# One Exp and a Newton step for the recurrence's 1/(1+t), and Tanh for all gate sigmoids but one

## The chip, the cores and the metric

The kernel runs on one core of one Trainium2 chip. The metric is device time in microseconds for one execution, 943.13 us as the median of three runs before the change (942.66 to 943.2). The core's engines each have a queue that goes in order: PE multiplies matrices (its weight loads, PEld, run beside it), ACT (ScalarE) evaluates activation functions and copies, DVE (VectorE) does elementwise work, POOL (GpSimd) small operations, SP issues the DMA transfers.

## The reference

A trunk of two layers over 512 positions of width 1024, all in float32. The first ("even") layer projects x once and feeds two branches: eight heads of retention and eight blocks of an RG-LRU recurrence. Each is multiplied by a SiLU gate. The second ("odd") layer is differential attention. The part that matters here:

```python
    ret = ((ret - mu) * lax.rsqrt(var + NORM_EPS)).reshape(B, S, RET_WIDTH) * gn_g + gn_b
    ret = ret * jax.nn.silu(g_ret.astype(jnp.float32))
    lru = rg_lru_branch(xb, conv_w, conv_b, wa, ba, wx, bx, lam) * jax.nn.silu(g_lru.astype(jnp.float32))
...
    r = jax.nn.sigmoid(jnp.einsum('bsgi,gij->bsgj', xg, wa).reshape(B, S, W) + ba)
    i = jax.nn.sigmoid(jnp.einsum('bsgi,gij->bsgj', xg, wx).reshape(B, S, W) + bx)
    log_a = -LRU_C * r * jax.nn.softplus(-lam.astype(jnp.float32))
    a = jnp.exp(log_a)
    u = xc * i * jnp.sqrt(-jnp.expm1(2.0 * log_a))
```

followed by the scan h = a h + u along the positions.

## The kernel before

Every float32 matrix product is three products of a high and a low part (`mm3`): the high part of an operand is a cast on ACT (L145), the low part the difference on DVE (L146), and both have to be there before PE can use the operand. Weights come in pieces of 512 KB through two raw buffers: SP issues a transfer when the piece two before it has been split (its DVE operation, as w19l, is done), ACT and DVE split it (w21h, w21l), PE uses it.

The even layer runs over heads. For each head there are projections for the two gates (`gl`, `gr`), the recurrence's input (`xb`), and retention's q and k, each 24 products of 512 columns on PE. Between these products stand the small ones of the heads: retention's scores (`rs`, four per head), their product with v (`ro`), the GroupNorm's variance (`rv`, which reads the split square `rq`), and the recurrence's two gates (`pr` and `pi`, which read the split convolution `xc`). PE's and SP's order is the order of the program, with turns counted in `Side`; ACT's and DVE's order is laid out by the scheduler, by priorities and its own costs, and is fixed when the program is built. Scores and gates (`rs`, `pr`, `pi`) take turns in two PSUM banks, so a product waits until DVE or ACT has read the one two before it.

The recurrence writes a = exp(log_a) with t = tanh(-log_a / 2): a = (1 - t) / (1 + t) and sqrt(1 - a^2) = 2 sqrt(t) / (1 + t). Its steps on ACT are Sigmoid (L491, into `t`), Sigmoid (L495, into `xbp`), Tanh (L497), Ln of 1 + t (L502), Exp of its negative (L503), Sqrt of t (L506); DVE sharpens 1/(1+t) by a Newton step (L504, L505) and goes on with L507 to L510, the last being the scan. The GroupNorm takes Ln (L461), Exp (L462) and a Square (L463). The gates take a Sigmoid (L408) and a product (L409). Where a function is not in the table set that ACT has loaded, an ACT_TABLE_LOAD stands ahead of it under the same line.

Of the kernel before, what the change touches and what calls it, by code (L numbers as in the profile page):

```python
# [95 lines left out]
def trunk(ctx: ExitStack, tc: tile.TileContext, a):  # L96
# [27 lines left out]
    def temp(name):  # L124
        return es.tile([P, S], F32, tag="es", name=name)
# [247 lines left out]
    conv_w = lambda i, c: vecs[:, i, c:c + 1]  # L373
    conv_b = lambda c: vecs[:, 4, c:c + 1]
    gba = lambda c: vecs[:, 5, c:c + 1]
    gbx = lambda c: vecs[:, 6, c:c + 1]
    gn = load("gn", [P, 2, KT], a["gn"])
    gng = const.tile([P, KT], F32, tag="gng", name="gng")
    nc.vector.tensor_scalar(out=gng, in0=gn[:, 0], scalar1=-0.5, scalar2=None, op0=ALU.mult)
    sg = load("sg", [P, 2], a["subln"])  # L380
    nc.vector.tensor_scalar(out=sg, in0=sg, scalar1=1.0 - LAMBDA_INIT, scalar2=None, op0=ALU.mult)
    cos = load("cos", [P, S], a["cos"])
# [48 lines left out]
    def retention(h, q, k, v, dec, m):  # L431
# [26 lines left out]
        with tc.high_priority(P_GROUP):  # L458
            sd = temp(f"rsd{h}")

            nc.scalar.activation(out=sq, in_=pv, func=AF.Ln, bias=epsb)  # L461
            nc.scalar.activation(out=sd, in_=sq, func=AF.Exp, scale=-0.5)  # L462
            nc.scalar.activation(out=sq, in_=sd, func=AF.Square)  # L463
            nc.vector.scalar_tensor_tensor(out=sq, in0=pv, scalar=EPS, in1=sq, op0=ALU.add, op1=ALU.mult)
            nc.vector.scalar_tensor_tensor(out=sd, in0=sq, scalar=3.0, in1=sd, op0=ALU.subtract, op1=ALU.mult)
            n1 = sq
            nc.vector.tensor_tensor(out=n1, in0=ps, in1=sd, op=ALU.mult)
            nc.vector.tensor_scalar(out=n1, in0=n1, scalar1=gng[:, h:h + 1], scalar2=gn[:, 1, h:h + 1], op0=ALU.mult, op1=ALU.add)
        if ("gr", h) not in gates:
            yield lambda: ("gr", h) in gates  # L470
        nc.vector.tensor_tensor(out=n1, in0=n1, in1=gates.pop(("gr", h)), op=ALU.mult)
# [2 lines left out]
    def lru(c, ps, m):  # L474
# [17 lines left out]
        pi = bank(ps_sc, "sc", f"pi{c}")  # L492
        mm3(pi, cut(gw[0], ALL, slice(o + P, o + 2 * P)), t2, True, True)
        i = xb
        nc.scalar.activation(out=i, in_=pi, func=AF.Sigmoid, bias=gbx(c))  # L495

        nc.scalar.activation(out=t, in_=t, func=AF.Tanh, scale=sp4[:, c:c + 1])  # L497
        nc.vector.tensor_tensor(out=i, in0=i, in1=xc, op=ALU.mult)  # L498
        d = xc
        r = temp(f"r{c}")  # L500

        nc.scalar.activation(out=r, in_=t, func=AF.Ln, bias=1.0)  # L502
        nc.scalar.activation(out=r, in_=r, func=AF.Exp, scale=-1.0)  # L503
# [29 lines left out]
    for kind, i in ev:  # L533
# [256 lines left out]
```

## Time and profile before

| what | value |
|---|---|
| median of the runs | 943.13 us |
| the profiled execution | 943.21 us |
| its span | 941.4 us |
| PE busy | 923.9 us, 98% |
| DVE busy | 692.7 us, 74% |
| ACT busy | 463.6 us, 49% |
| share of PE in the chain that ended last | 64% |
| share of DVE, of ACT in that chain | 19%, 8% |

The span is what the profiler recorded of the program's instructions, and 1.8 us of the execution lie outside of it. The even layer takes the first 400 us or so, the odd layer the rest. Times in rows are from the span's start.

### The profile page before, as it was taken

What the parts mean: (1) busy time and instruction counts of PE and PEld (TensorE: products, weight loads), DVE (VectorE), ACT (ScalarE), POOL (GpSimd) and SP (SyncE); (2) the same over time, 40 slices, a digit from 0 to 9 for tenths busy, and PEclk for the clock granted to TensorE, in tenths of its full rate; (3) what the DMA queues carried; (4) which work ended last, traced back from release to release, by engine and by line L of the source; (5) the groups of instructions that cost most, each with busy time, mean ns of one, the idle gap of its engine ahead of it and who ended that gap; (6) DMA issues with size and microseconds to landing.
All of it is one profiled execution on the core that took longest, in us unless ns stands there. A gap on an engine that the chain in (4) does not pass through costs nothing.

```text
span 941.4 us, 11566 instructions
## 1 busy us (share of the span) xinstructions
PE 923.9 (98%) x4327; PEld 764.8 (81%) x4327; DVE 692.7 (74%) x1171; ACT 463.6 (49%) x750; POOL 58.6 (6%) x118
## 2 busy tenths in 40 slices
PE   9999999999999999999999999999999999999996
PEld 7888888878887887888887888888788888887885
DVE  5877997868779988994489854478844488636777
ACT  5567786566374776423334454233453234444340
POOL 0000000000000000000001210100100001101023
PEclk9999999999999999999999999999999999999998
DMA  6562221512314123314221222042223142223102
GB/s 225 174 218 68 90 73 54 165 57 93 120 54 148 57 90 118 120 29 162 93 89 65 69 89 90 23 134 90 68 68 90 45 135 68 73 85 113 66 23 91
DMA packets 27418, 88.95 MB, mean 94 GB/s; under 512 B 3425, under 2 KB 3553, under 8 KB 27361
## 3 DMA queue, kind: packets, MB, share of 16 engines
q1 hardware_dynamic: 27360, 88.20, 28.6%
q8 instruction: 34, 0.56, 0.2%
q14 instruction: 24, 0.19, 0.1%
HBM read 86.09 MB, written 2.10 MB: 94 GB/s over the span
## 4 chain that ended last, share of the span: by engine, by line
PE 64%; DVE 19%; ACT 8%; issue 4%; DMA 2%; POOL 2%; SPq 0%; DVEq 0%; ACTq 0%; POOLq 0%
PE ov_ps L150 3%; PE ov_ps L151 3%; PE ov_ps L149 3%; PE og_ps L149 3%; PE og_ps L150 3%; PE og_ps L151 3%; PE ev_ps L149 2%; PE ev_ps L150 2%; PE oo_ps L149 2%; PE oo_ps L150 2%; PE oo_ps L151 2%; PE ev_ps L151 2%; ACT e L610 1%; PE xb_ps L149 1%; PE xb_ps L150 1%
## 5 line engine op out<-in xcount | busy, mean ns | idle before, releaser
L610 ACT ACTIVATE e<-as,nm 128x128 f32<-128x128 f32 (+3 forms) x64 | 33.2, 523 | 29.2 <-DVE nm L607 28.8
L641 DVE SCALAR_TENSOR_TENSOR o<-po,ars,og 128x256 f32<-128x256 f32 x32 | 15.5, 484 | 39.8 <-POOL ars L326 39.8
L607 DVE CUSTOM_DVE_ANT_0 as<-as,mask 128x128 f32<-128x128 f32 (+3 forms) x64 | 30.2, 510 | 1.9 <-PE as L151 1.9
L617 POOL TENSOR_SCALAR zr<-z 128x1 f32<-128x1 f32 x32 | 11.3, 352 | 309.9 <-ACT e L610 309.9
L325 POOL TENSOR_SCALAR rs_t<-bmv 128x1 f32<-128x1 f32 x6 | 2.3, 376 | 418.4 <-DVE bmv L336 418.4
L637 ACT ACTIVATE po<-po 128x256 f32<-128x256 f32 x32 | 11.8, 370 | 29.8 <-PE po L151 25.9
L325 POOL TENSOR_SCALAR rs_t<-ss,zr 128x1 f32<-128x1 f32 x32 | 16.0, 501 | 140.5 <-ACT po L637 135.5
L239 DVE TENSOR_TENSOR y<-oo_ps,y 128x512 f32<-128x512 f32 x24 | 16.3, 684 | 4.2 <-PE oo_ps L151 4.2
L326 POOL TENSOR_TENSOR ars<-rs_t,nhalf 128x1 f32<-128x1 f32 x32 | 18.9, 591 | 2.7
L482 DVE SCALAR_TENSOR_TENSOR xc<-xbp,vecs,xc 128x509 f32<-128x509 f32 (+2 forms) x24 | 17.9, 746 | 1.5 <-ACT xc L479 1.3
L618 DVE SCALAR_TENSOR_TENSOR e<-e,zr,e 128x128 f32<-128x128 f32 (+3 forms) x32 | 17.6, 551 | 1.0
L439 DVE TENSOR_TENSOR rsd<-rs,dec 128x512 f32<-128x512 f32 (+3 forms) x32 | 15.5, 486 | 1.1 <-PE rs L151 1.0
L615 DVE RECIPROCAL zr<-z 128x1 f32<-128x1 f32 x32 | 5.2, 162 | 15.1 <-ACT e L610 14.9
L646 PEld LDWEIGHTS po<-ident,o 128*128 128x128 f32 x64 | 8.3, 140 | 7.8 <-DVE o L641 4.8
L646 PE MATMUL po<-ident,o 128*128 128x128 f32 x64 | 12.6, 278 | 1.6 <-DVE o L641 1.4
L622 PE MATMUL wt<-ident,e 128*128 128x128 f32 x80 | 14.0, 272 | 0.0
L145 ACT CAST hh<-ht 128x512 fp32r<-128x512 f32 x8 | 4.7, 588 | 18.4 <-PE ht L577 18.4
L622 PEld LDWEIGHTS wt<-ident,e 128*128 128x128 f32 x80 | 10.4, 140 | 3.8 <-DVE e L618 0.4
L498 DVE TENSOR_TENSOR xbp<-xbp,xc 128x512 f32<-128x512 f32 x8 | 5.5, 690 | 9.9 <-ACT xbp L495 9.9
L610 ACT ACTIVATION_READ_ACCUMULATOR e<-as,nm 128x1 f32 x64 | 12.5, 196 | 0.0
L504 DVE SCALAR_TENSOR_TENSOR xc<-t,r 128x512 f32<-128x512 f32 x8 | 5.5, 691 | 9.0 <-ACT r L503 9.0
L408 ACT ACT_TABLE_LOAD x9 | 11.5, 1283 | 0.8 <-PE gl_ps L151 0.7
(2673 smaller groups left out, 3416.3 us busy)
## 6 DMA issues: line engine op xcount, KB each, us to landing
w_r<-in_od_w SPq DMA_DIRECT2D x64, 512.0 KB, 3.3
w_r<-in_ev_w SPq DMA_DIRECT2D x47, 512.0 KB, 3.3
w_r<-in_ev_wo SPq DMA_DIRECT2D x16, 512.0 KB, 3.4
w_r<-in_od_wo SPq DMA_DIRECT2D x16, 512.0 KB, 3.3
dec<-in_dec SPq DMA_DIRECT2D x8, 256.0 KB, 3.9
y<-in_x SPq DMA_DIRECT2D x4, 512.0 KB, 6.8
out_h<-y SPq DMA_DIRECT2D x8, 256.0 KB, 2.1
xr<-in_xt SPq DMA_DIRECT2D x3, 512.0 KB, 6.7
```

Of the source, the lines that this page charges most:

```text
L149: nc.tensor.matmul(out=out, lhsT=l[0], rhs=r[0], start=start, stop=False)
L150: nc.tensor.matmul(out=out, lhsT=l[0], rhs=r[1], start=False, stop=False)
L151: nc.tensor.matmul(out=out, lhsT=l[1], rhs=r[0], start=False, stop=stop)
L239: nc.vector.tensor_tensor(out=yy, in0=ps, in1=yy, op=ALU.add)
L325: nc.gpsimd.tensor_scalar(out=t, in0=var, scalar1=scale, scalar2=eps, op0=ALU.mult, op1=ALU.add)
L326: nc.gpsimd.tensor_tensor(out=out, in0=t, in1=nhalf[:, :1], op=ALU.pow)
L482: nc.vector.scalar_tensor_tensor(out=xc[:, sh:], in0=xb[:, :S - sh], scalar=conv_w(w, c), in1=xc[:, sh:], op0=ALU.mult, op1=ALU.add)
L607: nc.vector.tensor_tensor_reduce(out=ps[:, :n], in0=ps[:, :n], in1=mask[:, S - n:], scale=-QK_SCALE, scalar=3.0e38, op0=ALU.add, op1=ALU.m ...
L610: nc.scalar.activation(out=e, in_=ps[:, :n], func=AF.Exp, scale=-1.0, bias=nm, accum_out=z[:, mp:mp + 1])
L618: nc.vector.scalar_tensor_tensor(out=ee[0], in0=ee[1], scalar=zr[:, 0:1], in1=ee[0], op0=ALU.mult, op1=ALU.add)
L622: nc.tensor.transpose(out=pt[:, kb * P:kb * P + P], in_=ee[0][:, kb * P:kb * P + P], identity=ident)
L646: nc.tensor.transpose(out=pm[:, i * P:i * P + P], in_=o[:, i * P:i * P + P], identity=ident)
```

## The change

The gates' SiLU, x sigmoid(x), becomes x (1 + tanh(x/2)), which is twice of it; the factor of two is taken out of the GroupNorm's scale and offset (`gng`, `gnb`) and of the recurrence's factor (-2 becomes -0.5, with the one of the input gate `i`, which is formed in the same way, as (1 + tanh) xc). The recurrence's own gate stays a Sigmoid. The start of the Newton step for 1/(1+t), which was exp(-ln(1+t)), becomes (1 + exp(-2 sp4 r)) / 2, which is the same number: an Exp of the Sigmoid's output, scaled, and a Copy that halves it and adds a half. Three small tiles (`sp8`, `gbx2`, `gnb`) are made at the start.

```diff
-    nc.vector.tensor_scalar(out=gng, in0=gn[:, 0], scalar1=-0.5, scalar2=None, op0=ALU.mult)
+    nc.vector.tensor_scalar(out=gng, in0=gn[:, 0], scalar1=-0.25, scalar2=None, op0=ALU.mult)
...
-    def silu(ps, out, name):
+    sp8 = const.tile([P, KT], F32, tag="sp8", name="sp8")
+    nc.vector.tensor_scalar(out=sp8, in0=sp4, scalar1=-2.0, scalar2=None, op0=ALU.mult)
+    gbx2 = const.tile([P, KT], F32, tag="gbx2", name="gbx2")
+    nc.vector.tensor_scalar(out=gbx2, in0=vecs[:, 6], scalar1=0.5, scalar2=None, op0=ALU.mult)
+    gnb = const.tile([P, KT], F32, tag="gnb", name="gnb")
+    nc.vector.tensor_scalar(out=gnb, in0=gn[:, 1], scalar1=0.5, scalar2=None, op0=ALU.mult)
+
+    def silu2(ps, out, name):
+
         s = work(name + "_sg")
-        nc.scalar.activation(out=s, in_=ps, func=AF.Sigmoid)
-        nc.vector.tensor_tensor(out=out, in0=ps, in1=s, op=ALU.mult)
+        nc.scalar.activation(out=s, in_=ps, func=AF.Tanh, scale=0.5)
+        nc.vector.scalar_tensor_tensor(out=out, in0=s, scalar=1.0, in1=ps, op0=ALU.add, op1=ALU.mult)
...
-        nc.scalar.activation(out=i, in_=pi, func=AF.Sigmoid, bias=gbx(c))
-
+        nc.scalar.activation(out=i, in_=pi, func=AF.Tanh, scale=0.5, bias=gbx2[:, c:c + 1])
+
+        r = temp(f"r{c}")
+        nc.scalar.activation(out=r, in_=t, func=AF.Exp, scale=sp8[:, c:c + 1])
         nc.scalar.activation(out=t, in_=t, func=AF.Tanh, scale=sp4[:, c:c + 1])
-        nc.vector.tensor_tensor(out=i, in0=i, in1=xc, op=ALU.mult)
+        nc.vector.scalar_tensor_tensor(out=i, in0=i, scalar=1.0, in1=xc, op0=ALU.add, op1=ALU.mult)
         d = xc
-        r = temp(f"r{c}")
-
-        nc.scalar.activation(out=r, in_=t, func=AF.Ln, bias=1.0)
-        nc.scalar.activation(out=r, in_=r, func=AF.Exp, scale=-1.0)
+
+        nc.scalar.activation(out=r, in_=r, func=AF.Copy, scale=0.5, bias=0.5)
...
-        nc.vector.scalar_tensor_tensor(out=r, in0=r, scalar=-2.0, in1=d, op0=ALU.mult, op1=ALU.mult)
+        nc.vector.scalar_tensor_tensor(out=r, in0=r, scalar=-0.5, in1=d, op0=ALU.mult, op1=ALU.mult)
```

Lines after the new ones move by six. What the queues hold changes at places far from the diff, since the scheduler lays ACT and DVE out anew. Before, on ACT at head 2's recurrence: xc2h is the high part of the convolution, which PE's `pr` reads; w21h that of a weight piece for the output product; r12h and r13h those of retention's scores.

```order
L145 CAST w20h<-w_r 128x1024
L145 CAST r12h<-rsd_1028 128x256
L408 ACTIVATE gr_sg<-gr_ps 128x512
L145 CAST xc2h<-xc_1006 128x512
L145 CAST w21h<-w_r 128x1024
L145 CAST r13h<-rsd_1063 128x128
L491 ACTIVATE t_1088<-pr_1084,vecs 128x512
L497 ACTIVATE t_1088<-t_1088,sp_183 128x512
L495 ACTIVATE xbp_1004<-pi_1090,vecs 128x512
L502 ACT_TABLE_LOAD
L502 ACTIVATE r_1097<-t_1088 128x512
```

With the change, at the same place on ACT:

```order
L145 CAST w20h<-w_r 128x1024
L414 ACTIVATE gr_sg<-gr_ps 128x512
L145 CAST r12h<-rsd_1034 128x256
L145 CAST w21h<-w_r 128x1024
L145 CAST xc2h<-xc_1012 128x512
L145 CAST r13h<-rsd_1069 128x128
L497 ACT_TABLE_LOAD
L497 ACTIVATE t_1094<-pr_1090,vecs 128x512
L504 ACT_TABLE_LOAD
L504 ACTIVATE r_1101<-t_1094,sp_212 128x512
L501 ACTIVATE xbp_1010<-pi_1096,gbx_214 128x512
L505 ACTIVATE t_1094<-t_1094,sp_183 128x512
```

The cast w21h has moved ahead of xc2h, and the gate's Sigmoid has a table load of its own.

Before, on ACT at head 7's recurrence: `rq` is the square of the sixth head's GroupNorm, k7h the high part of the seventh head's k.

```order
L491 ACT_TABLE_LOAD
L491 ACTIVATE t_3007<-pr_3003,vecs 128x512
L495 ACTIVATE xbp_2910<-pi_3009,vecs 128x512
L497 ACTIVATE t_3007<-t_3007,sp_183 128x512
L461 ACT_TABLE_LOAD
L461 ACTIVATE rq_2988<-rv_3032,epsb 128x512
L502 ACTIVATE r_3016<-t_3007 128x512
L462 ACT_TABLE_LOAD
L462 ACTIVATE rsd_3035<-rq_2988 128x512
L145 CAST k7h<-k_c 128x512
L503 ACTIVATE r_3016<-r_3016 128x512
```

With the change, at the same place on ACT:

```order
L497 ACT_TABLE_LOAD
L497 ACTIVATE t_3013<-pr_3009,vecs 128x512
L501 ACTIVATE xbp_2916<-pi_3015,gbx_214 128x512
L504 ACT_TABLE_LOAD
L504 ACTIVATE r_3020<-t_3013,sp_212 128x512
L467 ACT_TABLE_LOAD
L467 ACTIVATE rq_2994<-rv_3038,epsb 128x512
L505 ACT_TABLE_LOAD
L505 ACTIVATE t_3013<-t_3013,sp_183 128x512
L145 CAST k7h<-k_c 128x512
L509 ACTIVATE r_3020<-r_3020 128x512
L468 ACTIVATE rsd_3041<-rq_2994 128x512
```

The GroupNorm's Ln stands between the recurrence's Exp and Tanh, so that three loads lie between the first gate activation and k7h, where there were two.

## Rows read from the trace of the kernel before

**Rows 1.** The page's first lines: the span, and for each engine its busy time, share of the span and instructions.

```profile
span 941.4 us, 11566 instructions
PE 923.9 (98%) x4327; PEld 764.8 (81%) x4327; DVE 692.7 (74%) x1171; ACT 463.6 (49%) x750; POOL 58.6 (6%) x118
```

**Rows 2.** The window from 20 to 400 us (busy time of PE, PEld, DVE, ACT, POOL, the granted clock, the DMA share, GB/s), and four of the seven rows of PE's waits in that window (total, times, longest, in us).

```profile
20.00:400.00 380.00, 377.19 (x1708) 312.59 (x1707) 316.52 (x482) 242.82 (x318) 2.17 (x2) 1.00 0.32 105
...
PE pi L149 <- DVE rsd L439: 0.9, 1, 0.9
PE rv L456 <- ACT rq7h L145: 0.5, 1, 0.5
...
PE rv L457 <- DVE rq7l L146: 0.2, 1, 0.2
...
PE rv L457 <- DVE rq1l L146: 0.2, 1, 0.2
```

**Rows 3.** DVE and PE in order of time at the start: the first two are the last of the small operations on the recurrence's constants and the low part of the fourth weight piece, then PE's last product that does without that part and the first that reads it (start, duration).

```profile
22.88 0.17 DVE L404 SCALAR_TENSOR_TENSOR sp<-sb__185,sc 128x8 f32<-128x8 f32 x1
22.96 1.22 DVE L146 TENSOR_TENSOR w3l<-w_r,w3h 128x1024 fp32r<-128x1024 f32 x1
...
24.23 0.39 PE L149 MATMUL ev_ps<-w3h,xh 128*128 128x512 f32 x1
24.46 0.39 PE L150 MATMUL ev_ps<-w3l,xh 128*128 128x512 f32 x1
```

**Rows 4.** Groups of ACT's instructions by line up to 480 us, and one of DVE's (count, busy time, mean ns of one, idle time before them and what ended it).

```profile
L462 ACT ACT_TABLE_LOAD x8 | 10.3, 1283 | 0.1
...
L497 ACT ACTIVATE t<-t,sp 128x512 f32<-128x512 f32 x8 | 5.8, 723 | 0.2
...
L462 ACT ACTIVATE rsd<-rq 128x512 f32<-128x512 f32 x8 | 5.1, 632 | 0.1
...
L504 DVE SCALAR_TENSOR_TENSOR xc<-t,r 128x512 f32<-128x512 f32 x8 | 5.5, 691 | 9.0 <-ACT r L503 9.0
```

**Rows 5.** ACT, DVE, PE and SP in order of time around head 2's recurrence (start, duration, in brackets the idle time before it and what ended it), and the page's row on the transfers of the output weights (count, KB, median us from issue to landing).

```profile
112.47 0.62 ACT L145 CAST xc2h<-xc 128x512 fp32r<-128x512 f32 x1 [0.80 <-DVE xc L482]
113.48 1.05 ACT L145 CAST w21h<-w_r 128x1024 fp32r<-128x1024 f32 x1 [0.39 <-DMA w_r<-in_ev_wo]
...
121.89 0.60 ACT L145 CAST rq1h<-rq 128x512 fp32r<-128x512 f32 x1
...
108.04 1.23 DVE L146 TENSOR_TENSOR w19l<-w_r,w19h 128x1024 fp32r<-128x1024 f32 x1 [0.34 <-ACT w19h L145]
...
113.13 0.69 DVE L146 TENSOR_TENSOR xc2l<-xc,xc2h 128x512 fp32r<-128x512 f32 x1
...
122.53 0.69 DVE L146 TENSOR_TENSOR rq1l<-rq,rq1h 128x512 fp32r<-128x512 f32 x1 [1.27 <-ACT rq1h L145]
...
113.57 0.39 PE L149 MATMUL pr<-xc2h,gw2h 128*128 128x512 f32 x1
113.88 0.50 PE L150 MATMUL pr<-xc2l,gw2h 128*128 128x512 f32 x1
...
122.55 0.51 PE L456 MATMUL rv<-rq1h,ones 128*128 128x512 f32 x1
123.28 0.50 PE L457 MATMUL rv<-rq1l,ones 128*128 128x512 f32 x1 [0.22 <-DVE rq1l L146]
...
109.29 0.33 SPq L171 DMA_DIRECT2D w_r<-in_ev_wo  x1
...
w_r<-in_ev_wo SPq DMA_DIRECT2D x16, 512.0 KB, 3.4
```

**Rows 6.** ACT, DVE and PE in order of time from head 6's to head 7's GroupNorm, and the window from k7l to w59l with the same columns as in rows 2.

```profile
328.95 1.04 ACT L145 CAST w55h<-w_r 128x1024 fp32r<-128x1024 f32 x1
...
345.13 0.69 ACT L491 ACTIVATE t<-pr,vecs 128x512 f32<-128x512 f32 x1
345.72 0.68 ACT L495 ACTIVATE xbp<-pi,vecs 128x512 f32<-128x512 f32 x1
...
351.38 0.60 ACT L145 CAST k7h<-k_c 128x512 fp32r<-128x512 f32 x1
...
372.85 1.05 ACT L145 CAST w61h<-w_r 128x1024 fp32r<-128x1024 f32 x1 [5.72 <-DMA w_r<-in_ev_wo]
...
352.02 0.69 DVE L146 TENSOR_TENSOR k7l<-k_c,k7h 128x512 fp32r<-128x512 f32 x1 [1.59 <-ACT k7h L145]
...
366.21 1.22 DVE L146 TENSOR_TENSOR w59l<-w_r,w59h 128x1024 fp32r<-128x1024 f32 x1
...
373.93 1.23 DVE L146 TENSOR_TENSOR w61l<-w_r,w61h 128x1024 fp32r<-128x1024 f32 x1 [3.96 <-ACT w61h L145]
375.07 0.69 DVE L146 TENSOR_TENSOR rq7l<-rq,rq7h 128x512 fp32r<-128x512 f32 x1
...
374.19 0.39 PE L151 MATMUL ro_ps<-w59h,retm2l 128*128 128x512 f32 x1
375.09 0.49 PE L456 MATMUL rv<-rq7h,ones 128*128 128x512 f32 x1 [0.51 <-ACT rq7h L145]
375.82 0.50 PE L457 MATMUL rv<-rq7l,ones 128*128 128x512 f32 x1 [0.23 <-DVE rq7l L146]
...
352.00:367.40 15.40, 15.40 (x73) 12.91 (x72) 15.38 (x26) 12.84 (x18) 0.00 (x0) 1.00 0.18 57
```

More of the change, by code (lines that the diff above doesn't have):

```diff
@@ L375, in trunk @@
     gba = lambda c: vecs[:, 5, c:c + 1]
-    gbx = lambda c: vecs[:, 6, c:c + 1]
     gn = load("gn", [P, 2, KT], a["gn"])
     gng = const.tile([P, KT], F32, tag="gng", name="gng")
-    nc.vector.tensor_scalar(out=gng, in0=gn[:, 0], scalar1=-0.5, scalar2=None, op0=ALU.mult)
+    nc.vector.tensor_scalar(out=gng, in0=gn[:, 0], scalar1=-0.25, scalar2=None, op0=ALU.mult)
     sg = load("sg", [P, 2], a["subln"])
@@ L467, in retention @@
             nc.vector.tensor_tensor(out=n1, in0=ps, in1=sd, op=ALU.mult)
-            nc.vector.tensor_scalar(out=n1, in0=n1, scalar1=gng[:, h:h + 1], scalar2=gn[:, 1, h:h + 1], op0=ALU.mult, op1=ALU.add)
+            nc.vector.tensor_scalar(out=n1, in0=n1, scalar1=gng[:, h:h + 1], scalar2=gnb[:, h:h + 1], op0=ALU.mult, op1=ALU.add)
         if ("gr", h) not in gates:
@@ L557, in trunk @@
             g = gp.tile([P, S], F32, tag="g", name=f"{kind}{i}")
-            silu(ps, g, f"{kind}{i}")
+            silu2(ps, g, f"{kind}{i}")
             gates[kind, i] = g
```

## The prediction

> **What bounds the kernel now.** I read the page's first two lines, then the idle time of TensorE (PE) by window and by releaser, and only then the engines that the change touches. PE is busy for 923.9 of 941.4 us [rows 1], and its granted clock is full in the stretch that the change touches: from 20 to 400 us it is busy for 377.19 of 380 us at 1.00 [rows 2]. So this stretch, where the retention and RG-LRU heads run, offers 2.8 us of idle PE; by the starts of PE's instructions against their pace, 0.23 us (24.23 to 24.46 [rows 3]), I count a little over 4. Four of the seven waits are in rows 2; none has ScalarE's table loads (ACT) named as releaser. PE and the DMA queue keep their order (their two sequences are the same before and after); ACT and VectorE (DVE) get a new one. An engine's queue goes in order, so I follow the new queues where they feed a PE instruction that has little slack. A measurement of this kernel tells 0.2% from no change, about 1.9 us.
>
> **The change part by part.** ACT's table loads go from 60 to 54 (counted in the two queues), each 1.283 us [rows 4]: 6 x 1.283 = 7.7 us less on an engine that is busy for 463.6 of 941.4 us [rows 1]. None of that is on PE's path, so I count it as nothing in itself; its cover is PE's own 98%. The other ACT work is traded one for one: Sigmoid for Tanh, Ln for Exp, Exp for Copy. No row has the new Tanh of PSUM or the new Copy; the nearest are 0.723 (the old Tanh, L497) and 0.632 us (L462's Exp) [rows 4]. Per gate the sum differs from the old one by less than 0.1 us either way, and I take 0. The same for DVE: the gate products become scalar_tensor_tensor, 0.691 us in L504's row [rows 4] against the old products' 0.69.
>
> The Trainium skill (ScalarE: Activation LUTs, "What ACT_TABLE_LOAD costs") charges a further 1.38 us of drain to every switch of set. By it the six loads would be worth 16 us of ACT time; in rows 4 the load is 1.283 us and L462's eight loads had 0.1 us of idle before them in all, so the trace shows no such drain. What that rule would do to the time is the last rival.
>
> *The start: +0.1.* Three small DVE operations are new, ahead of the cast of w3l. L404, of their kind, takes 0.17 us and the next one starts 0.08 later [rows 3]. Two of the three can overlap (0.08 each), the third depends on its forerunner (0.20): 0.36 together. w3l now ends at 22.96 + 1.22 = 24.18, PE reads it at 24.46 [rows 3]: slack 0.28, so PE loses 0.08. Bounds 0 (all overlap) to 0.35.
>
> *Place A, head 2's gate input: +0.5.* Before, ACT casts xc2h at 112.47 and then w21h at 113.48, which waited for its weights; DVE's xc2l starts at 113.13, and PE takes xc2h at 113.57 and xc2l at 113.88, just as it is ready [rows 5]. Now w21h stands ahead of xc2h. If its weights land when they did, w21h runs from 113.48 for 1.05, xc2h from about 114.45 for 0.62, xc2l from 115.1 for 0.69, and PE's second matmul starts at 115.85 rather than 113.88: +1.97. But the transfer of w21 is issued when w19l is done (108.04 + 1.23 = 109.27, issue at 109.29) [rows 5], and this DVE queue should be ahead of its old time: it used to wait 9.0 us in eight heads, 1.1 each, for the second Exp of the old reciprocal [rows 4], which no longer has a load of its own. Laid out from head 1's rows I get about 0.85 us, so +1.1. Were the transfer also to take the median of the page, 3.4 us, not the 4.2 between 109.29 and 113.48, another 0.8 goes and +0.3 is left [rows 5]. Bounds +0.3 and +2.0; I take +1.1, since nothing in the order makes the transfer faster.
>
> Behind it PE used to wait for rq1l: its two matmuls start 0.73 apart (122.55, 123.28), 0.50 more than the pace [rows 2, 5]. rq1h depends on PE's ro and on ACT; ACT now has one load where it had two between the gate and rq1h, rq1h comes at about its old 121.9 to 122.3 and rq1l by 123.2, while PE arrives at 123.9 [rows 5]. So this wait goes: -0.5, with -0.1 for the matmul after it. Sum of A: 1.1 - 0.6 = +0.5, bounds -0.3 and +1.4.
>
> *Place B, head 7: +1.0.* Between ACT's first gate activation and the cast of k7h there were two table loads and there are three, since the GroupNorm's Ln now stands between the gate's Exp and its Tanh. From the rows: the gate starts at 345.13, the next activation ends at 345.72 + 0.68 = 346.40 [rows 6]; then load 1.28, Exp 0.72, load 1.28, Ln 0.69, load 1.28, each with 0.02 behind it, put the Tanh at 351.74 and k7h 0.6 later at 352.3. It was 351.38: +0.95. PE itself has slack there. But DVE's k7l waits for k7h (1.59 us of idle before it at 352.02) and from there DVE has no gap, 15.38 of 15.40 us busy [rows 6]. Its operations up to w59l are the same ones in another order, so w59l (366.21) slips by the same 1.0. What is queued behind w59l: the transfer of w61 is issued at its end, w61h waits for that landing (5.72 us of idle before 372.85), DVE's w61l and rq7l follow w61h, and PE waits for rq7l at 375.82 [rows 6]. The square that makes rq7 moves ahead of w61h, which makes rq7h earlier against w61h but not rq7l, since w61l is ahead of it. So PE's second rv matmul goes from 375.82 to 376.8: +1.0. Bounds: 0, if the transfer, queued behind three others, lands no later; +2.0, if k7h slips further (below). I take +1.0 by the rows.
>
> The other waits stay: pi for rsd [rows 2], ro for r31l and for r53l hang on chains that start at a PE end and hold no moved operation. The odd layer's queues are the same, and it starts from the same state.
>
> *Sum.* 0.1 + 0.5 + 1.0 = +1.6 on a span of 941.4: 943.0, and 944.8 with the 1.8 us that lie around it in the profiled run of 943.21. That run is 0.1 above the median, so on the median 943.13 + 1.6 = 944.7 us.
>
> **The rivals.**
> *Nothing arrives (943.0).* The transfer of w21 lands in 3.4 us (A: 0.3 - 0.6 = -0.3) and the slip at B is eaten because w61's landing is set by the three transfers ahead of it, not by its issue. For it: 5.72 us of wait is long against 3.4, so the queue in front counts [rows 5, 6]. Against: those three wait on the same DVE stretch. Sum -0.2.
> *Faster (941.2).* Both rv waits that the changed ACT queue feeds go: rq1's 0.6 and rq7's. The second loses 375.09 - 374.19 - 0.23 = 0.67 and 375.82 - 375.09 - 0.23 = 0.50, 1.2 together [rows 6]. Sum -1.9. Against: A and B are both shown in the queues, and with only some 4 us of waits in the stretch there is no more to gain.
> *Slower (945.6).* B in full. The cast w55h (1.04 us) now stands ahead of the GroupNorm's square and of r60h on ACT [rows 6]; where its transfer is just in time, DVE's queue slips by some 0.5 already from 329 us, and so does the gate at 345.13. k7h is then 1.5 late, the scores' read rsd is late by as much, and PE's next score has to wait for its bank too: B costs +1.9. With A's +0.5 and the start's 0.1 the sum is +2.5. It decides from k7h later than 352.6.
> *The page's drain (946.1).* If a switch costs 2.66 us where sets really alternate, the third load in B costs 1.4 more: 944.7 + 1.4. Rows 4 speak against it.
>
> **How the numbers follow.** Forecast (+0.6 to +1.9 us, all but its upper end within 0.2%) 0.34; nothing arrives 0.26; slower 0.27; the page's drain 0.02; faster 0.08; 0.03 for what I don't see, split. Faster by over 0.2% takes over half of the rival and some of the rest: 0.06. Slower by over 0.2%: the slower rival, the drain, the upper end of the forecast (0.06) and 0.02: 0.37. Within: 0.57. Time 944.7; the range that leaves a tenth on either side goes from 942.5 (below "nothing arrives") to 946.4 (above "slower", A at its bound).
>
> **What would show it.** Right at A: new waits of pr for xc2h (ACT) and xc2l (DVE), about 1.1 us together at 114 us, none for rq1l, and w21h directly ahead of xc2h with idle before it that a transfer ends. Right at B: k7h some 1.0 later against PE's rs of head 7, w61h again behind a transfer, rv's two starts later by 1.0 against the ro matmul ahead of them. ACT busy less by 7 to 8 us, DVE's the same. Wrong: xc2h not waiting; the rv of head 7 at once behind its ro matmul; or a wait in the odd layer that is not there now.

## The result, and the profile after

The changed kernel takes 945.0 us as the median of 16 runs (943.9 to 947.71), the kernel before beside it 943.12 (942.66 to 943.52): ratio 1.0023, 95% interval 1.0015 to 1.003, so slower by 1.9 us. The profiled execution took 944.25 us, 1.04 above the 943.21 of before, with a span of 942.4. It is the second fastest of the 16 runs, so its rows hold 1.0 of the 1.9 us.

The page's first lines, as in [rows 1]:

```profile
span 942.4 us, 11562 instructions
PE 922.5 (98%) x4327; PEld 762.9 (81%) x4327; DVE 693.0 (74%) x1174; ACT 455.2 (48%) x744; POOL 57.6 (6%) x118
```

ACT has 8.4 us less to do, the kernel takes longer. The groups of ACT's loads up to 480 us, as in [rows 4], show what became of them: Exp and Tanh share a load (L505 has one load for eight Tanhs), and the one is where Ln stands between them, at head 7.

```profile
L497 ACT ACT_TABLE_LOAD x8 | 10.3, 1283 | 0.1
L504 ACT ACT_TABLE_LOAD x8 | 10.3, 1283 | 0.1
...
L505 ACT ACT_TABLE_LOAD x1 | 1.3, 1283 | 0.0
```

The window from 20 to 400 us and all rows of PE's waits in it, as in [rows 2]:

```profile
20.00:400.00 380.00, 376.13 (x1702) 311.45 (x1701) 315.41 (x480) 234.34 (x311) 1.29 (x2) 1.00 0.32 105
PE rs L149 <- DVE rsd L445: 0.9, 2, 0.6
PE rv L463 <- DVE rq7l L146: 0.9, 1, 0.9
PE rv L462 <- ACT rq7h L145: 0.6, 1, 0.6
PE ro L150 <- DVE r31l L146: 0.5, 1, 0.5
PE pi L149 <- DVE rsd L445: 0.4, 1, 0.4
PE pr L149 <- ACT xc2h L145: 0.3, 1, 0.3
PE ro L150 <- DVE r53l L146: 0.2, 1, 0.2
PE pr L150 <- DVE xc2l L146: 0.2, 1, 0.2
```

PE is busy for 1.06 us less of this window. New are pr's waits for xc2 and a second wait at rs. Those at rv for rq7 have grown from 0.5 and 0.2 to 0.6 and 0.9, those for rq1l are gone, and pi's has gone from 0.9 to 0.4.

Place A, head 2, ACT, DVE and PE in order of time, as in [rows 5]:

```profile
112.35 1.05 ACT L145 CAST w21h<-w_r 128x1024 fp32r<-128x1024 f32 x1 [1.60 <-DMA w_r<-in_ev_wo]
113.31 0.61 ACT L145 CAST xc2h<-xc 128x512 fp32r<-128x512 f32 x1
...
112.53 1.22 DVE L146 TENSOR_TENSOR w20l<-w_r,w20h 128x1024 fp32r<-128x1024 f32 x1
113.95 0.69 DVE L146 TENSOR_TENSOR xc2l<-xc,xc2h 128x512 fp32r<-128x512 f32 x1 [0.20 <-ACT xc2h L145]
...
113.97 0.50 PE L149 MATMUL pr<-xc2h,gw2h 128*128 128x512 f32 x1 [0.30 <-ACT xc2h L145]
114.70 0.50 PE L150 MATMUL pr<-xc2l,gw2h 128*128 128x512 f32 x1 [0.22 <-DVE xc2l L146]
...
123.32 0.40 PE L462 MATMUL rv<-rq1h,ones 128*128 128x512 f32 x1
123.56 0.39 PE L463 MATMUL rv<-rq1l,ones 128*128 128x512 f32 x1
```

ACT stood idle for 1.60 us in front of w21h, whose weights had not landed, while xc was nearly ready behind it. PE's second pr matmul is 0.82 later than before (113.88). The two rv matmuls are now at pace (0.24 apart, 0.73 before). DVE holds something I had not read in its queue: w20l, 1.22 us long, has moved ahead of xc2l as well.

Place B, head 7, as in [rows 6], with SP's transfers (the w_r at 368.86 is w61):

```profile
350.54 1.28 ACT L505 ACT_TABLE_LOAD   x1
351.83 0.72 ACT L505 ACTIVATE t<-t,sp 128x512 f32<-128x512 f32 x1
352.46 0.61 ACT L145 CAST k7h<-k_c 128x512 fp32r<-128x512 f32 x1
...
367.35 1.22 DVE L146 TENSOR_TENSOR w59l<-w_r,w59h 128x1024 fp32r<-128x1024 f32 x1
...
364.35 0.33 PE L149 MATMUL rs<-q7h,k7h 128*128 128x128 f32 x1 [0.59 <-DVE rsd L445]
...
367.46 1.29 SPq L155 DMA_DIRECT2D ln<-in_ev_ln  x3
368.86 0.36 SPq L171 DMA_DIRECT2D w_r<-in_ev_wo  x1
...
373.98 1.05 ACT L145 CAST w61h<-w_r 128x1024 fp32r<-128x1024 f32 x1 [1.76 <-DMA w_r<-in_ev_wo]
...
376.21 0.69 DVE L146 TENSOR_TENSOR rq7l<-rq,rq7h 128x512 fp32r<-128x512 f32 x1
...
375.60 0.50 PE L462 MATMUL rv<-rq7h,ones 128*128 128x512 f32 x1 [0.55 <-ACT rq7h L145]
376.95 0.51 PE L463 MATMUL rv<-rq7l,ones 128*128 128x512 f32 x1 [0.85 <-DVE rq7l L146]
```

k7h is 1.08 later, w59l 1.14, w61h 1.13, and PE's second rv matmul 1.13 (375.82 before). From there PE keeps its distance to the end.

SP does not issue w61 at the end of w59l (368.57). Three of the four ln transfers, the layer norm's scale and offset, stand ahead of it in SP's queue. They wait for DVE's last read of the scores (rsd, directly ahead of w59l), and w61 follows them, 0.29 behind w59l's end. In the kernel before, w61 is issued 0.28 behind it (the first of the three w_r is w61):

```profile
366.32 1.28 SPq L155 DMA_DIRECT2D ln<-in_ev_ln  x3
367.71 7.80 SPq L171 DMA_DIRECT2D w_r<-in_ev_wo  x3
```

Set against the starts of the same PE instructions before, the shift is -0.05 ahead of A, +0.82 at pr, +0.18 behind rv of head 1, -0.33 at pi, +0.46 at rs of head 7, +1.13 at its rv, and +1.0 at the end.

### The profile page after: what moved, and what is told of

It reads as the page before. It is cut to its first block, busy times and chain, and to the rows that moved or that the text cites. A ratio compares the mean times of both kernels' runs of the same rounds, so it can differ in the third digit from the quotient of the medians.

```text
span 942.4 us, 11562 instructions
## 1 busy us (share of the span) xinstructions
PE 922.5 (98%) x4327; PEld 762.9 (81%) x4327; DVE 693.0 (74%) x1174; ACT 455.2 (48%) x744; POOL 57.6 (6%) x118
## 4 chain that ended last, share of the span: by engine, by line
PE 71%; DVE 16%; ACT 4%; issue 3%; DMA 2%; POOL 2%; SPq 0%; DVEq 0%; ACTq 0%; POOLq 0%
PE ov_ps L151 3%; PE ov_ps L150 3%; PE ov_ps L149 3%; PE og_ps L149 3%; PE og_ps L150 3%; PE og_ps L151 3%; PE oo_ps L149 2%; PE oo_ps L150 2%; PE oo_ps L151 2%; PE out_ps L149 2%; PE out_ps L150 2%; PE out_ps L151 2%; DMA w_r<-in_ev_w 2%; ACT e L616 1%; PE ev_ps L150 1%
## 5 line engine op out<-in xcount | busy, mean ns | idle before, releaser
L145 ACT CAST hh<-ht 128x512 fp32r<-128x512 f32 x8 | 4.7, 589 | 18.0 <-PE ht L583 18.0
L356 DVE SCALAR_TENSOR_TENSOR y<-y,bmv,ln 128x512 f32<-128x512 f32 x14 | 11.1, 820 | 0.1
```

## The experiments

The scheduler lays the queues of ACT and DVE out anew whenever the program changes, so an order was put back by a dependency that orders two instructions of one queue (`issue_after`, `add_manual_dep`). Where "the queues are held", the whole order of ACT and DVE was fixed in this way, and only the swap that is shown differs. Each kernel ran beside the kernel before, on the same chip. Line numbers differ between the kernels: L145, L214 and L227 are the same cast on ACT.

**1. xc2h ahead of w21h.**

```diff
-        split(raw[:, c], cut(w, ALL, c), scale=scale)
+        if n == 21:
+            with tc.issue_after(marks["xc", 2].ins):
+                split(raw[:, c], cut(w, ALL, c), scale=scale)
+        else:
+            split(raw[:, c], cut(w, ALL, c), scale=scale)
```

> The changed kernel with one thing put back: on ACT the cast xc2h stands ahead of w21h again; no other instruction of any queue moves. Theory 1 (the loss is made of the two places where PE-critical casts stand behind casts that wait for weights): PE's waits of 0.30 and 0.22 us for xc2h and xc2l at 114 us go, the shift of PE against the kernel before goes from +0.83 back to about 0 there, no wait for rq1l takes its place (rq1l at about 121.4 us, PE at 122.5), and as DVE is released by PE between 189 and 262 us, the 0.3 to 0.8 us stay gained behind pi's wait at 305 us: 944.2 to 944.7, median against 945.0. Theory 2 (the loss comes with the new instruction forms or with the gate's own table load, wherever the casts stand): 945.0. Theory 3 (the wait of pi for rsd takes up whatever PE gains before it): the wait at pi grows from 0.39 to about 1.0 and the time stays 945.0. On the spread (943.9 to 947.7 in 16 runs after, 942.7 to 943.5 before): if the landing of w21 makes it, it falls to about 1 us here.

945.0 us (ratio 1.0022, 1.0013 to 1.0031): nothing gained. DVE and PE at 113 us say why:

```profile
112.74 1.22 DVE L146 TENSOR_TENSOR w20l<-w_r,w20h 128x1024 fp32r<-128x1024 f32 x1
113.87 0.69 DVE L146 TENSOR_TENSOR xc2l<-xc,xc2h 128x512 fp32r<-128x512 f32 x1
...
114.62 0.50 PE L151 MATMUL pr<-xc2l,gw2h 128*128 128x512 f32 x1 [0.52 <-DVE xc2l L146]
```

xc2h was ready at 113.00, and xc2l stood behind w20l. The cause was half read: two casts had moved, not one. The runs still spread over 2.0 us, not the 1 us expected.

**2. rq7 ahead of w61.** w61h and w61l behind rq7h and rq7l, by the same means; the scheduler then laid out anew what follows 376 us.

```diff
+                if n == 61:
+                    with tc.issue_after(marks["rq", 7][0].ins), tc.issue_after(marks["rq", 7][1].ins):
+                        split(raw[:, c], cut(w, ALL, c), scale=scale)
```

> The changed kernel, with w61h and w61l issued behind rq7h and rq7l on ACT and DVE; k7h, the three loads ahead of it and all before 366 us stay, some small operations behind 376 us change places. Theory 1 (PE's 1.4 us of waiting at the seventh head's rv is the landing of w61 handed on through w61h and w61l, which stand ahead of rq7h and rq7l): both rv waits (0.55 and 0.85) go, w61h still waits for its transfer at 374 us, the rest stays: 943.5 to 943.8 against 945.0. Rival (rq7 is late by itself, because the square or the DVE queue is late): rv still waits by 0.5 us or more, 944.5 or above. Rival (w61l is needed by PE soon behind it, the wait only moves on): rv's waits go, and a wait for w61 of about 1 us comes, 945.0. On the spread: if the landing of w61 makes it, it falls to about 1 us here.

944.56 us (1.0017, 1.0008 to 1.0026). Both rv waits are gone, but PE then waits 0.90 us for y (DVE L244, behind w62l) and 0.30 for w63l. The second rival came true in kind: the wait moved on. (The profiled run is the slowest of its eleven, 945.58 us.)

**3. The recurrence's Tanh ahead of the GroupNorm's Ln.**

```diff
-            nc.scalar.activation(out=sq, in_=pv, func=AF.Ln, bias=epsb)
+            with tc.issue_after(marks["t", 7].ins) if h == 6 else ExitStack():
+                nc.scalar.activation(out=sq, in_=pv, func=AF.Ln, bias=epsb)
```

> The changed kernel with the GroupNorm's Ln of head 6 issued behind the recurrence's Tanh of head 7 on ACT; the scheduler then also puts w58h and w58l ahead of k7h and k7l, and rq7h and rq7l ahead of w61h and w61l; before 345 us nothing moves. One load instead of two stands between the gate's Exp and k7h. Theory 1: k7h at about 350.2 us rather than 352.46, DVE's stretch behind it 1 to 2 us earlier, the wait of PE's last score of head 7 for its bank (0.59) gone, rv's two waits gone: 942.7 to 943.3 against 945.0, which is this place's whole +1.5 and the 0.7 that was there before. Rival (DVE's stretch is set by its own work, not by k7h): rs still waits by 0.3 us or more and the time is that of the kernel with rq7 put first, 943.6.

944.31 us (1.0016, 1.0007 to 1.0025). k7h came at 351.12 although PE was 1.1 later there by A (w21 took 4.4 us to land in this run), but DVE put r73l ahead of w59l, w61h came only at 374.78, and PE waited 1.21 for y and 0.33 for w63l. Of 2.0 expected, 0.4 to 0.7 arrived. The verdict on B is open after this one, as the scheduler moved too much.

**4. The Tanh half alone.** All gates in the new form, 1/(1+t) again by Ln and Exp.

```diff
-        nc.scalar.activation(out=r, in_=t, func=AF.Exp, scale=sp8[:, c:c + 1])
         nc.scalar.activation(out=t, in_=t, func=AF.Tanh, scale=sp4[:, c:c + 1])
...
-        nc.scalar.activation(out=r, in_=r, func=AF.Copy, scale=0.5, bias=0.5)
+        nc.scalar.activation(out=r, in_=t, func=AF.Ln, bias=1.0)
+        nc.scalar.activation(out=r, in_=r, func=AF.Exp, scale=-1.0)
```

> Only the Tanh half of the change: all gate Sigmoids but one are Tanh, with their scales and the three small operations at the start, and 1/(1+t) starts again from Ln and Exp. Table loads are 60, as before the change. At both places the casts stand as before the change (xc2h ahead of w21h; two loads between the gate and k7h). Theory 1 (places alone): 943.0 to 943.4, as before, with the old waits (rq1l 0.2, rv 0.5 and 0.2, pi 0.9). Theory 2 (Tanh from PSUM or the products as scalar_tensor_tensor cost something on the way to PE): 943.8 to 944.5. ACT busy about the 463.6 us of before.

944.62 us (1.0018, 1.001 to 1.0027). Theory 1 failed: the casts stand as before, and the time is that of the whole change. PE shows a new wait at head 2, with ACT ahead of it:

```profile
114.65 1.28 ACT L497 ACT_TABLE_LOAD   x1
...
123.19 0.60 ACT L145 CAST rq1h<-rq 128x512 fp32r<-128x512 f32 x1
...
123.85 0.50 PE L462 MATMUL rv<-rq1h,ones 128*128 128x512 f32 x1 [0.80 <-ACT rq1h L145]
```

The gate's Sigmoid (L497) needs a load of its own now that the others are Tanh. With the two loads of Ln and Exp still there, rq1h is 1.3 later, of which 0.4 is PE's later start in this run. In the whole change one of those is gone, which covers it. So the number of loads (60, as before) does not decide, but which load stands ahead of a cast that PE waits for. That the new forms cost nothing by themselves is seen only in experiment 9, which has them all and is level with the kernel before.

**5. Both parts of xc2 first.** xc2h ahead of w21h and xc2l ahead of w20l; nothing else moves.

```diff
+                if n in (20, 21):
+                    behind(marks["xc", 2], cast if n == 21 else (None, cast[1]))
```

> The changed kernel with both parts of xc2 ahead of the weights: xc2h ahead of w21h on ACT, and xc2l ahead of w20l on DVE; nothing else of any queue moves. Theory 1 (place A is two swaps, and in the kernel with xc2h alone put first the other one, w20l with its 1.2 us ahead of xc2l, still held PE): no wait of pr above 0.15 us, PE's shift against the kernel before at 115 us is only that of the start (0 to 0.4), the rv of head 1 waits for nothing, and 0.8 to 1.2 us of it reach the end: 0.7 to 1.1 above the kernel before, where the changed kernel is 1.9 above. Theory 3 (pi's wait for rsd at 305 us takes up what PE gains before it, since DVE does not come earlier): the wait at pi grows by what was gained, to 1.0 us or more, and the time stays 1.9 above.

943.56 us against 943.1 (1.0003, 0.9995 to 1.0012). No wait at pr, and pi's wait stays at 0.39, so theory 3 falls. Place A is worth about 1.4 us, more than the 0.8 to 1.2 expected.

**6. Ln ahead of Exp, queues held.** ACT at head 7:

```diff
 ACT_TABLE_LOAD
-ACTIVATE r<-t,sp 128x512
-ACT_TABLE_LOAD
-ACTIVATE rq<-rv,epsb 128x512
-ACT_TABLE_LOAD
+ACTIVATE rq<-rv,epsb 128x512
+ACT_TABLE_LOAD
+ACTIVATE r<-t,sp 128x512
 ACTIVATE t<-t,sp 128x512
```

> The changed kernel with every queue of ACT and DVE held in its order, but for one swap: on ACT the GroupNorm's Ln of head 6 stands ahead of the recurrence's Exp of head 7, so that Ln, Exp and Tanh need two table loads and not three (53 in all). Theory 1 (place B is the third load, handed on through DVE's full stretch to w59l, w61's transfer and rq7l): k7h 1.3 us earlier against the gate's activation, the wait of rs for its bank (0.59) gone, w59l and w61h 1.1 to 1.3 earlier, rv's second matmul too: 0.5 to 0.9 above the kernel before, where the changed kernel is 1.9 above. Rival (DVE's stretch is paced by PE's scores or by the transfers, and the load is hidden): w59l and w61h at their old distance, 1.6 to 1.9 above.

943.8 us against 943.1 (1.0012, 1.0003 to 1.0021): 1.2 of the 1.9 us go with this one load. k7h starts at 351.08, 5.97 behind the gate instead of 7.24, and w61h at 372.57. By these rows the rival falls. The median alone says less: three of the eleven runs are still 2.4 to 3.4 us above the kernel before.

**7. The small operations on GpSimd.**

```diff
-    nc.vector.tensor_scalar(out=sp8, in0=sp4, scalar1=-2.0, scalar2=None, op0=ALU.mult)
+    nc.gpsimd.tensor_scalar(out=sp8, in0=sp4, scalar1=-2.0, scalar2=None, op0=ALU.mult)
...
-    nc.vector.tensor_scalar(out=gbx2, in0=vecs[:, 6], scalar1=0.5, scalar2=None, op0=ALU.mult)
+    nc.gpsimd.tensor_scalar(out=gbx2, in0=vecs[:, 6], scalar1=0.5, scalar2=None, op0=ALU.mult)
...
-    nc.vector.tensor_scalar(out=gnb, in0=gn[:, 1], scalar1=0.5, scalar2=None, op0=ALU.mult)
+    nc.gpsimd.tensor_scalar(out=gnb, in0=gn[:, 1], scalar1=0.5, scalar2=None, op0=ALU.mult)
```

> The changed kernel with the three small operations of the start (sp8, gbx2, gnb) on GpSimd; ACT's and DVE's order is otherwise the same. In the five profiles with these operations on DVE, the cast w3l starts 6.92 to 6.99 us behind the landing of the last piece of xr, and 6.51 in the kernel before. Theory S (they cost PE 0.3 us on the average, not the 0.1 forecast): w3l at 6.5 to 6.6 behind that landing, 1.5 to 1.7 above the kernel before, where the changed kernel is 1.9 above. Rival (PE's start is set by the transfers): 1.9.

945.25 us (1.0021, 1.0012 to 1.003). w3l starts 6.65 us behind the landing, as theory S had it, yet nothing is gained: PE's shift behind w3l is +0.40 here too. In the other profiles it lies between -0.4 and +0.6, in no order that follows the edits, and moving the three operations away did not lower it. So they set nothing there.

**8. The Newton half alone.** 1/(1+t) in the new form, all gates by Sigmoid again.

```diff
-        nc.scalar.activation(out=i, in_=pi, func=AF.Tanh, scale=0.5, bias=gbx2[:, c:c + 1])
+        nc.scalar.activation(out=i, in_=pi, func=AF.Sigmoid, bias=gbx(c))
...
-        nc.scalar.activation(out=s, in_=ps, func=AF.Tanh, scale=0.5)
-        nc.vector.scalar_tensor_tensor(out=out, in0=s, scalar=1.0, in1=ps, op0=ALU.add, op1=ALU.mult)
+        nc.scalar.activation(out=s, in_=ps, func=AF.Sigmoid)
+        nc.vector.tensor_tensor(out=out, in0=ps, in1=s, op=ALU.mult)
```

> Only the other half of the change: 1/(1+t) starts from one Exp and a Copy, all gates keep their Sigmoids. 58 table loads, one small operation at the start instead of three. xc2h stands ahead of w21h, xc2l ahead of w20l, rq7h ahead of w61h; between the gate and k7h stand three loads. Theory 1 (time follows the few places, not the count of loads or ACT's busy time): the waits at pr, rq1l and rv are gone, the third load at head 7 still makes DVE's stretch late, and the late weights end it: between 0.3 below and 0.8 above the kernel before. Theory 4 (each load that goes is worth something): two of six loads gone, hardly a difference, but the sign of the changed kernel: 0.3 to 0.8 above. If it is 1.5 or more above, the places at heads 2 and 7 that I read are not what the time is made of.

947.2 us (1.0045, 1.0032 to 1.0057), far outside all that was expected, though pr and rv hardly wait. ACT and PE:

```profile
378.42 1.05 ACT L145 CAST w61h<-w_r 128x1024 fp32r<-128x1024 f32 x1 [3.25 <-DMA w_r<-in_ev_wo]
...
391.60 0.50 PE L149 MATMUL eo_ps<-w63h,retm3h 128*128 128x512 f32 x1 [1.00 <-ACT retm3h L145]
```

In this DVE queue more operations stand between k7h and w59l (18.07 us from one to the other, 14.89 in the changed kernel). w59l is at 371.28, so w61 is issued at 372.57 and lands 5.6 later than in the kernel before. On ACT head 7's GroupNorm stands behind w61h, and PE waits for its end. So the place is head 7 again, but here DVE's order makes w59l late, and rq7 stands ahead of w61. What it has in common with the other kernels is the landing of w61.

**What the traces have in common.** The start of w61h (it follows the landing within 0.1) and of the second rv matmul, in the nine kernels in which PE waits at rv for an rq7l that stands behind w61l:

| kernel | w61h | rv | distance |
|---|---|---|---|
| before | 372.85 | 375.82 | 2.97 |
| after | 373.98 | 376.95 | 2.97 |
| 1 | 373.89 | 376.86 | 2.97 |
| 4 | 373.95 | 376.93 | 2.98 |
| 5 | 372.83 | 375.79 | 2.96 |
| 6 | 372.57 | 375.53 | 2.96 |
| 7 | 374.56 | 377.53 | 2.97 |
| 9 (below) | 372.88 | 375.84 | 2.96 |
| 11 (below) | 373.57 | 376.54 | 2.97 |

From rv to the end of the span it is 565.5 to 565.9 us in all nine. So in these nine the landing of w61 fixes the time, and whatever comes ahead of it counts only as far as it moves that landing. (Kernel 12 has the same order; there PE does not wait at rv.)

**9. A and B together, queues held.** The swaps of 5 and 6.

> The changed kernel with the queues of ACT and DVE held, but for the swaps of the two experiments that gained: xc2h ahead of w21h, xc2l ahead of w20l, and the GroupNorm's Ln of head 6 ahead of the recurrence's Exp of head 7. Theory 1 (the loss is the two places, and they add up): 1.4 and 1.2 us less than the changed kernel's 1.9 above, so 0.4 to 1.0 below the kernel before, with runs within 1.5 us of each other. Rival (they share a wait, as each frees what the other hides): 0.3 above to 0.3 below.

942.93 us against 942.97 (1.0001, 0.9992 to 1.001). The whole loss is gone. That is 1.9 us where 1.4 and 1.2 would make 2.6, and falls among the rival's numbers; but the interval of each of these gains is some 0.8 us or more to either side, so the 0.7 between them is not clear of noise. ACT, PE and SP:

```profile
372.88 1.05 ACT L227 CAST w61h<-w_r 128x1024 fp32r<-128x1024 f32 x1 [1.97 <-DMA w_r<-in_ev_wo]
...
374.50 0.50 PE L544 MATMUL rv<-rq7h,ones 128*128 128x512 f32 x1 [0.77 <-ACT rq7h L227]
375.84 0.50 PE L545 MATMUL rv<-rq7l,ones 128*128 128x512 f32 x1 [0.85 <-DVE rq7l L228]
...
365.68 1.82 SPq L237 DMA_DIRECT2D ln<-in_ev_ln  x3
367.61 0.36 SPq L253 DMA_DIRECT2D w_r<-in_ev_wo  x1
```

Each swap alone brings w61h back to 372.6 or 372.8. Both together bring it no further in this profile, and PE waits off at rv what it had gained. Up to w59l, however, the two do add:

| kernel | ACT's gate activation, head 7 | from there to k7h | from k7h to w59l | w59l |
|---|---|---|---|---|
| after | 345.22 | 7.24 | 14.89 | 367.35 |
| 5 | 344.17 | 7.25 | 14.89 | 366.31 |
| 6 | 345.11 | 5.97 | 14.89 | 365.97 |
| 9 | 344.70 | 5.98 | 14.88 | 365.56 |

A moves the gate, B the way from the gate to k7h, and the rest is the same. Two things eat the sum in this run. The gate comes 0.5 later than in 5, since PE started 0.2 later and lost 0.3 more at rv of head 1. And SP took 1.82 us for three ln issues (1.28 in 6; one of them took 0.98 us, 0.43 in 6), so w61 was issued 0.83 behind the end of w59l instead of 0.29. That the two share a wait is therefore not shown.

**10. Three further swaps, queues held.** In DVE's queue (and rq7h ahead of w61h on ACT):

```diff
-TENSOR_TENSOR q_s<-q_ps,sin 64x512
 TENSOR_TENSOR rsd<-rs,dec 128x384
+TENSOR_TENSOR q_s<-q_ps,sin 64x512
...
+TENSOR_TENSOR r53l<-rsd,r53h 128x128
 SCALAR_TENSOR_TENSOR t<-t,xc 128x512
 SCALAR_TENSOR_TENSOR r<-r,xc 128x512
-TENSOR_TENSOR r53l<-rsd,r53h 128x128
...
+TENSOR_TENSOR rq7l<-rq,rq7h 128x512
 TENSOR_TENSOR w61l<-w_r,w61h 128x1024
-TENSOR_TENSOR rq7l<-rq,rq7h 128x512
```

> The same, with three further swaps of neighbours, each taken from a wait of PE in the last profiles: rq7h and rq7l ahead of w61h and w61l (0.84 us of waiting at rv), the second score of head 5 (rsd) ahead of a step of the rope on DVE (0.39 at pi), r53l ahead of two steps of the recurrence (0.23 at ro). Nothing else moves, in contrast to the earlier kernel with rq7 put first, where the scheduler laid out anew what came behind. If the waits are what they seem: 1.0 to 1.4 us less than the kernel with the two places alone, 1.6 to 2.3 below the kernel before. Rival (what PE gains there it waits for in the next stage, for y or for w63l, as in the earlier kernel): 0.5 to 1.0 below.

941.62 us against 942.97 (0.9986, 0.9978 to 0.9995): faster than both kernels. PE's waits from 20 to 400 us, all of them:

```profile
PE ro L232 <- DVE r31l L228: 0.5, 1, 0.5
PE ro_ps L231 <- DVE gl L497: 0.4, 1, 0.4
PE rs L231 <- DVE rsd L527: 0.3, 1, 0.3
```

The time is 1.3 us below kernel 9, between the two expectations. With rq7 off the landing, rv starts at 372.08, 3.76 earlier than in 9, but the span is only 2.4 shorter: 1.3 is lost again by 390 us, which is what the rival said in part. What each of the three swaps gives is not shown, as they moved together.

**11. Place A's order in the kernel before.** The old arithmetic, with w21h ahead of xc2h and w20l ahead of xc2l.

```diff
+                if n in (20, 21):
+                    behind(cast if n == 21 else (None, cast[1]), marks["xc", 2] if n == 20 else marks["xc", 2][:1])
```

> The kernel before, its arithmetic unchanged, with place A's order taken over: w21h ahead of xc2h on ACT, w20l ahead of xc2l on DVE; nothing else moves. Theory 1 (the order costs, not the new forms): pr waits for xc2h and xc2l by 1.2 to 2.2 us at 114 us, more than in the changed kernel since the transfer of w21 is issued 0.5 later there; the old waits at rq1l and rv stay; 1.0 to 1.9 above the kernel before, and runs spread over more than 2 us, since the landing of w21 (3.1 to 4.4 us from its issue in the profiles so far) now reaches PE. Rival (part of what A cost in the changed kernel was its new gate load): 0.3 to 0.8 above.

944.28 us against 942.97 (1.0015, 1.0006 to 1.0024). pr waits 0.41 and 0.29 and w61h comes at 373.57. Two swaps in the order, with no new form of instruction, cost 1.3 us. The stall was smaller than expected, since w21 landed earlier in this run (w21h at 112.66).

**12. w61 ahead of ln.** Queues of ACT, DVE and PE held; only SP's order changes.

```diff
 DMA ident<-in_ident 128x128
+DMA w_r<-in_ev_wo 128x1024
+DMA w_r<-in_ev_wo 128x1024
+DMA w_r<-in_ev_wo 128x1024
 DMA ln<-in_ev_ln 128x512
...
-DMA w_r<-in_ev_wo 128x1024
-DMA w_r<-in_ev_wo 128x1024
-DMA w_r<-in_ev_wo 128x1024
```

> The changed kernel with ACT, DVE and PE held in their order; only on SP the four transfers of the layer norm's scale and offset (ln) are issued behind those of w61, w62 and w63 instead of ahead of them. In eight profiles so far rv's second matmul started 3.0 us behind the landing of w61, and w61 landed 5.0 to 5.3 us behind its issue, with three ln transfers ahead of it. Theory F (up to 376 us the even layer's time is the landing of w61 and 3.0 us; the two places only move its issue): the issue stays at w59l's end (0.3 earlier), the landing is 3.2 to 3.6 us behind it and so about 2 us earlier, rv's waits of 0.55 and 0.85 go to 0 to 0.3, and the time is 0.3 to 0.9 above the kernel before, where the changed kernel is 1.9 above. Rival (the landing of w61 is set by something else than the ln transfers, or PE then waits for w63 or y by as much): 1.5 to 1.9 above.

943.15 us against 943.14 (1.0004, 0.9995 to 1.0013): the loss is gone, although xc2h stands behind w21h and three loads stand ahead of k7h. SP, ACT and PE:

```profile
368.50 0.33 SPq L240 DMA_DIRECT2D w_r<-in_ev_wo  x1
...
372.02 1.04 ACT L214 CAST w61h<-w_r 128x1024 fp32r<-128x1024 f32 x1
...
374.79 0.40 PE L531 MATMUL rv<-rq7h,ones 128*128 128x512 f32 x1
375.02 0.45 PE L532 MATMUL rv<-rq7l,ones 128*128 128x512 f32 x1
```

w61 is issued nearly when it was (368.86) and has landed by 371.90, 3.4 us later instead of 5.1. Neither w61h nor rv waits. PE still comes to rv 0.37 later than in the kernel before, so A and B are not undone; what it gains is the wait at rv, and the kernel before has 0.74 of that itself (0.51 and 0.23 [rows 6]). The same move in the kernel before wasn't tried.

## Why the prediction was right, and where it was not

**The number and its sign.** 944.7 was forecast, 945.0 came, inside the likeliest case's own bounds of +0.6 to +1.9 on the median, at their upper end. The 0.23% fall just into "slower by over 0.2%", which had 0.37; "within" had 0.57. "None of that is on PE's path" held: kernels with 54, 60 and 58 loads are 1.9, 1.75 and 4.1 us above the kernel before, and with 53 (3, 6, 9 and 10) 1.4 above, 0.7 above, level and 1.35 below it.

**The start, +0.1.** -0.05 in the profile; the three operations cost nothing that experiment 7 could find.

**Place A, +0.5.** The price was near: a stall of 0.87 in the profile with w21 landing in 3.6 us (w21h at 112.35), 1.3 to 1.6 ahead of rv in experiments 2 and 3, where it came at 113.28 and 113.41, for 1.1 forecast. The loss of the wait at rq1l came as worked out (0.64 for 0.6). The mechanism was half right: "now w21h stands ahead of xc2h" left out w20l ahead of xc2l on DVE, which alone held PE in experiment 1. That queue was in front of me and I read only ACT's.

**Place B, +1.0.** Each link came as named, and within 0.2 us: k7h 352.46 (352.3 forecast), w59l +1.14, the landing +1.13, rv +1.13. Experiments 6, 9 and 12 show the chain from both ends. One link is off: the transfer of w61 is not issued at w59l's end but behind the three ln issues, 0.28 later. That was so before, and changes nothing here; in the profile of 9 the slow issue costs 0.5. At rs, PE waited 0.59 for its bank, which I had left to the "slower" rival; it costs nothing extra, since rv waits for the landing anyway. By the Trainium skill (ScalarE: Activation LUTs, "What ACT_TABLE_LOAD costs") each of the loads between the gate and k7h would have cost 1.38 us more; there each load started 0.02 to 0.03 us behind the activation ahead of it, and each Exp, Ln and Tanh 0.01 us behind its load, so the trace doesn't agree.

**What was not right: the terms of the sum.** "Sum. 0.1 + 0.5 + 1.0" came near, but the profile adds up otherwise. "The other waits stay" failed at pi, whose wait fell from 0.87 to 0.39. With -0.05 at the start, +0.87 and -0.64 at A and -0.48 at pi, PE was 0.3 ahead of its old time behind pi and 0.4 at 326 us, where 0.6 behind was forecast. Then a third place took 0.47 back. DVE, which waits there for PE, starts at 325.85 (326.23 before). But ACT has w55h, which waits for its transfer, ahead of the GroupNorm's square, and DVE waits for that square:

```profile
325.85 0.69 DVE L239 TENSOR_TENSOR y<-lo_ps,y 128x512 f32<-128x512 f32 x1 [0.76 <-PE lo_ps L151]
...
327.84 1.05 ACT L145 CAST w55h<-w_r 128x1024 fp32r<-128x1024 f32 x1 [0.37 <-DMA w_r<-in_ev_w]
...
329.45 0.69 DVE L470 SCALAR_TENSOR_TENSOR rq<-rv,rq 128x512 f32<-128x512 f32 x1 [0.49 <-ACT rq L469]
...
345.22 0.69 ACT L497 ACTIVATE t<-pr,vecs 128x512 f32<-128x512 f32 x1
```

So head 7's gate starts 0.09 later than before, and B's third load adds 1.0 to that. The prediction had seen w55h and priced it at 0.5, but only in the "slower" rival. That the two terms left out of the sum, -0.5 and +0.5, cancel is luck. No run puts w55h back alone, so its price is read from the trace and not shown by an experiment. The median lies 0.75 above the profiled run; in experiments 2 and 3, where w21 landed later, the gate starts 1.1 to 1.2 later than before, which would cover it, but that is not shown run by run.

The path was too simple as well. The sum takes a delay of PE as one that stays to the end, but PE waits at rv for the landing of w61 whatever it had lost before. A reaches that landing only by way of DVE, which waits for PE at 326 us and from there sets the gate, k7h and w59l. In experiment 5 this path passes A on in full: against the changed kernel rv of head 1 is 1.03 earlier, the gate 1.05, w59l 1.04 and head 7's rv 1.16.

**The rivals.** "Nothing arrives" rested on w61's landing being "set by the three transfers ahead of it". They do lengthen it by 1.7 us, as experiment 12 shows, but they are issued by the same late DVE stretch, as I wrote against it. "Slower" named the slip at w55h and the bank wait rightly, but k7h came at 352.46, short of its 352.6, and the bank wait costs nothing behind rv.

**Open.** Why the runs spread over 3.8 us, where the kernel before spreads over 0.9 (16 runs) to 1.8 (33 runs). In the profiles w21 took 3.1 to 4.4 us from issue to landing. Kernels with xc2 behind w21h spread over 1.8 to 3.8 us (the changed kernel, 2, 3, 6, 7, 11, 12), those with both its parts ahead over 1.2 to 1.8 (4, 5, 8, 9, 10). That fits a landing that reaches PE at A; it isn't shown run by run, and the two groups touch. Open too is why one ln issue took 0.98 us on SP in 9, and whether A and B together gain less than one by one.

## What to carry to other kernels

Where a scheduler lays out the queues, a change of arithmetic is also a change of order: compare the new order on every engine that feeds the bounding one, at the few places without slack, before counting what the arithmetic saves. Find the wait at which the bounding engine meets a transfer's landing: a delay ahead of it counts only as far as it moves that landing, so follow it to the transfer's issue before adding it up. Casts that the bounding engine waits for belong ahead of casts that wait for a transfer, and transfers needed soon ahead of those needed late.

## What the runs showed of the hardware that was not expected

A transfer of 512 KB landed 5.1 us behind its issue with three others of 256 KB issued 0.5 to 1.4 us ahead of it, and 3.4 us behind it without them (experiment 12). The Trainium skill says that on each DMA engine descriptors are taken in the order of the ring (DMA: Bandwidth & Descriptors, "Queues, rings and completion order"), with which this agrees. The same transfer of w21, whose place in the queue did not change, took from 3.1 to 4.4 us in the fourteen profiles.
